# Two attention preparations ahead of the fourth GDN head, and an attend with two score banks, in a two-layer hybrid backbone

## The chip, the cores and the metric

The kernel runs on one core of one Trainium2 chip, as one program. The metric is the time of one execution in microseconds on the device; of several executions the median is taken. A core has five engines that each run their own instructions in order: TensorE (PE, and PEld for its weight loads), VectorE (DVE), ScalarE (ACT), GpSimd (POOL) and SyncE (SP), which here issues the DMAs. They wait for each other through semaphores.

## The reference

Two layers of a diffusion backbone on 1024 latent tokens and 256 context tokens of width 1024. Each layer normalises and modulates its input, mixes the tokens in three parallel groups of heads from one input projection into one output projection, and ends with an MLP of width 4096. The mixer, cut to what matters:

```python
pl = split_cols(h_lat @ w_in, IN_SIZES)        # and pc, of the context
# 4 GDN heads: chunked delta rule, forward and backward
sol = lax.linalg.triangular_solve(amat, rhs, lower=True, unit_diagonal=True)
...
S, o = lax.scan(step, s0, (u, w, attn, qg, kg, glast))
# RG-LRU, width 256, forward and backward: h = a*h + u along the tokens
a = jnp.exp(log_a);  u = jnp.sqrt(-jnp.expm1(2.0 * log_a)) * (i * xc)
# 4 attention heads with latent keys and values; context queries read context keys only
s = jnp.einsum('bqhd,bkhd->bhqk', q, k).astype(jnp.float32) * ((MLA_NOPE + MLA_ROPE) ** -0.5)
p = jax.nn.softmax(s, axis=-1)
y_lat = jnp.concatenate([gdn_out(...), rl * gelu(...), a_l], axis=-1) @ w_out
```

Context outputs of the mixer are computed in layer 0 only.

## The kernel before

All matrices lie with features on the partitions and tokens along the free axis. The tokens stand in three blocks: two of 512 latent tokens (0 and 1) and one of 256 context tokens ("c"). Most float32 products are made of three passes on a high and a low part (tiles "wh" and "wl").

`mixer` writes one layer's work in this order. After the projections for each group (`tiles(h)`: the keys, queries, values and gate of GDN head h), `head(h)` runs GDN head h; heads 0 to 2 are written among the projections. Then come `head(3)`, `mla_open` (the loads of what the attention shares), `mla_prep` 0, the LRU, `mla_prep` 1, `mla_attend` 0, `mla_prep` 2, `mla_attend` 1, `mla_prep` 3, the loads of the mixer's results, `mla_attend` 2 and 3, and the output projection.

- A **GDN head** has an opening (from L591: keys times keys and keys times queries, decays); `gdn_invert`, which inverts 32 x 32 triangles by 60 small VectorE operations on tiles X and T between two pairs of transposes (L681 to L690) and joins them by small matmuls; `gdn_scan`, a recurrence over ten chunks of 128 tokens in two directions, forward with PSUM bank "a" and backward with bank "b", whose last step is an addition to its output X from bank "c" (L790 is the last matmul); and `gdn_y`, which normalises (L821), and gates and stores the output.
- An **attention preparation** (`mla_prep`) computes head h's keys K, queries Q (with the rotary embedding), the row maxima of the scores (matmul L984, VectorE reduction L985, L987) and values V. Preparations 0 and 1 use banks "st" and "d", 2 and 3 "st" and "b". K and V have two buffers each, taken by h modulo 2.
- An **attend** (`mla_attend`) runs over two latent query blocks with ten key chunks each, and over the context block (two chunks) in layer 0. For each chunk there are three score matmuls (L1014 to L1016), an exponential on ScalarE, and a value matmul into bank "d" (L1029); at the end of a block there is a reciprocal (L1031). A score tile takes one of the two "mm" banks; every third one takes bank "a".
- Each chunk also calls `tick(1)`, which may do one step of work that has been put by: in layer 0 these are adaLN products that are needed behind the mixer (`ada_pe`, L273, in bank "c"), each with a load of 512 KB into the two-buffer tile "wr".
- The **LRU** (`lru`, from L826) has 20 segments of 256 tokens a layer: five token blocks, two halves of the width and two directions. A segment is a chain over ScalarE, VectorE and GpSimd: gate activations, an integer seed for an inverse square root (L862), two Newton steps that alternate between GpSimd and VectorE, and a scan instruction along the tokens (L875 forward, L878 backward) that begins from the last value of the segment before it. Its tiles ("lr", with 14 buffers of tag "L") lie in pool mp.

The order in which each engine gets its instructions isn't the order of the text. A scheduler takes, for each engine, what can go next by priority, and priority follows the order in which the program writes the work; `later()` puts back the counter behind a block, so that what follows the LRU has the same priorities as the LRU itself. So the LRU is mixed with whatever is written behind it. On the chip each engine runs its list in order.

```python
self.flip = (self.flip + 1) % 3
ps = (self.MM() if self.flip else self.PT("a"))[:, :n]
```

Of the kernel before, what the change touches and what calls it, by code (L numbers as in the profile page):

```python
# [43 lines left out]
class Trunk:  # L44
# [954 lines left out]
            self.act(V[:, c0:c0 + w, 0:64], ps[:, :w * 64].rearrange("p (c d) -> p c d", d=64))  # L999
        return K, Q, V  # L1000

    def mla_attend(self, h, kqv, with_ctx, yd):

        nc = self.nc
        K, Q, V = kqv
        sc = 96.0 ** -0.5
        hp = 64 * (h % 2)

        def scores(b, b2, i, p):
            n = BLK[b][1]  # L1010
            k = K[b2][:, :, i * P:(i + 1) * P]
            self.flip = (self.flip + 1) % 3
            ps = (self.MM() if self.flip else self.PT("a"))[:, :n]
            nc.tensor.matmul(ps, k[0:97, 0, :], Q[b][0:97, 0, :], start=True, stop=False)  # L1014
            nc.tensor.matmul(ps, k[0:96, 0, :], Q[b][0:96, 1, :], start=False, stop=False)
            nc.tensor.matmul(ps, k[0:96, 1, :], Q[b][0:96, 0, :], start=False, stop=True)  # L1016
            self.act(p, ps, AF.Exp, scale=sc)
        for b in [0, 1] + (["c"] if with_ctx else []):
            chunks = [(b2, i) for b2 in (BL if b != "c" else ["c"]) for i in range(GRP[b2][1])]
            s, n = BLK[b]  # L1020
            po = self.PT("d")[:, :n]
            for ci, (b2, i) in enumerate(chunks):
                c = GRP[b2][0] + i
                self.tick(1)
                if ci % 2 == 0:
                    pt = self.wp.tile([P, 2, 512], F32, tag=("wl", "wh")[ci // 2 % 2], bufs=2, name=self.nm("Pt"))
                p = pt[:, ci % 2, :n]
                scores(b, b2, i, p)
                nc.tensor.matmul(po, V[:, c, :], p, start=ci == 0, stop=ci == len(chunks) - 1)  # L1029
            rc = self.T()[0:64, :n]  # L1030
            nc.vector.reciprocal(rc, po[64:128, :])  # L1031
            self.tt(rc, po[0:64, :], rc, ALU.mult)
            nc.sync.dma_start(yd[hp:hp + 64, s:s + n], rc)

    def mixer(self, L, hs, obl):

        nc = self.nc
        l, last = L.l, L.l == DEPTH - 1
# [3 lines left out]
        yd = [self.dram(f"y{i}") for i in range(8)]  # L1042
# [36 lines left out]
        def head(h):  # L1079
            with self.actor("g", (gp, 2), ["c"]):  # L1080
                o = self.gdn_head(L, h, *kd[h], last)
                self.gdn_y(o, kd[h][1][1], zd[h], obl, yd[h])
# [23 lines left out]
        self.lw = mp.tile([P, 2, 2, 2, P], F32, name=self.nm("lw"))  # L1106
        nc.sync.dma_start(self.lw, self.I["lru_w"][l])
        mq = self.pool("mq", side)
        head(3)
        self.cur = ("s", (self.tp, 4), ["st", "d"])  # L1110
        self.mla_open(L, pk, mq, not last)
        kqv = [self.mla_prep(L, 0, mq, not last)]
# [2 lines left out]
            self.lru(L, [x for x, _ in xg], [g for _, g in xg], obl, yd[4:6])  # L1115
        self.cur = mine
        kqv.append(self.mla_prep(L, 1, mq, not last))
        self.cur = ("s", (self.tp, 4), ["st", "b"])
        self.mla_attend(0, kqv[0], not last, yd[6])
        kqv.append(self.mla_prep(L, 2, mq, not last))  # L1120
        self.mla_attend(1, kqv[1], not last, yd[6])
        kqv.append(self.mla_prep(L, 3, mq, not last))
# [316 lines left out]
```

## Time and profile before

| | |
|---|---|
| time, median of 3 runs (us) | 3834.12 (3833.47 to 3840.0) |
| profiled execution: time, span (us) | 3833.43, 3831.6 |
| mean granted TensorE clock | 0.958 |
| TensorE, VectorE, ScalarE, GpSimd busy | 91%, 55%, 43%, 34% |
| layer 0: head 3's L681, end of its scan, last attend's last reciprocal (us) | 630.5, 747, 1001 |
| layer 1: the same (us) | 2635.2, 2747, 2977 |

The span is divided by the profile into instructions with a start, a length, the engine, the line of the kernel, the operation, and the tiles (out<-in). A stretch's busy time is the union of an engine's instructions in it. An idle time before an instruction is shown in brackets with what ended it. Names of one letter or two are tiles; "lr" are all tiles of the LRU.

### The profile page before, as it was taken

The numbers are of one execution on the slowest core, as the hardware profiler recorded it, in microseconds if no ns is written. First come the engines' busy times: TensorE is split into PE (matmuls) and PEld (weight loads), VectorE is DVE, ScalarE is ACT, GpSimd is POOL, SyncE is SP. The second block draws the span as 40 slices with busy tenths as digits, with TensorE's granted clock in tenths as the row PEclk, the third lists the DMA queues.
The fourth block names the chain that finished last, engine by engine and source line by source line (L and its number), as shares of the span: only waits on it lengthen the run. The fifth ranks groups of instructions, "written<-read, shape, count | busy, mean of one in ns | idle before, by whom it ended". The sixth has DMA issues, their size and how long they took to land. (4 is left out here: it accounts for less than half of the span.)

```text
span 3831.6 us, 51475 instructions
## 1 busy us (share of the span) xinstructions
PE 3501.0 (91%) x19236; PEld 2746.6 (72%) x19236; DVE 2093.5 (55%) x4351; ACT 1645.2 (43%) x3477; POOL 1310.3 (34%) x919
## 2 busy tenths in 40 slices
PE   5999986898999999999997989897887999999998
PEld 3777774645787888888877777774544778888886
DVE  6666577756365155555256685677766361421224
ACT  3554544545454322122354454554555453222242
POOL 4212212235575211111465322112244674222254
PEclk9999998899999999999998999997998999999999
DMA  5221213151532222222434322212002432311143
GB/s 184 93 92 60 93 60 93 34 161 44 175 105 89 66 83 94 88 94 89 130 107 138 99 81 78 86 65 74 31 27 81 153 105 94 96 47 47 51 139 99
DMA packets 164922, 347.13 MB, mean 91 GB/s; under 512 B 15552, under 2 KB 74304, under 8 KB 164672
## 3 DMA queue, kind: packets, MB, share of 16 engines
q1 hardware_dynamic: 164672, 343.85, 27.7%
q8 instruction: 151, 2.47, 0.3%
q14 instruction: 99, 0.81, 0.1%
HBM read 277.99 MB, written 65.80 MB: 90 GB/s over the span
## 5 line engine op out<-in xcount | busy, mean ns | idle before, releaser
L138 POOL TENSOR_TENSOR wl<-wr,wh 128x1024 fp32r<-128x1024 f32 x280 | 682.4, 2438 | 1630.0 <-ACT wh L135 951.7
L230 PE MATMUL mm<-A,wh 128*128 128x512 f32 (+1 forms) x3008 | 704.3, 377 | 11.8 <-DVE A L138 5.4
L135 ACT ACTIVATE wh<-wr 128x1024 fp32r<-128x1024 f32 x288 | 304.9, 1059 | 855.5 <-PE mm L230 332.5
L230 PEld LDWEIGHTS mm<-A,wh 128*128 128x128 f32 x3008 | 521.6, 193 | 107.2 <-DVE A L138 7.3
L138 DVE TENSOR_TENSOR hid<-T,hid 128x512 fp32r<-128x512 f32 (+1 forms) x160 | 172.4, 1080 | 451.9 <-ACT hid L135 451.9
L230 PE MATMUL mm<-A,wl 128*128 128x512 f32 (+1 forms) x1504 | 353.5, 371 | 1.2 <-DVE wl L138 1.1
L230 PE MATMUL mm<-hid,wh 128*128 128x512 f32 (+1 forms) x1280 | 301.8, 377 | 8.8 <-ACT T L135 6.8
L230 PEld LDWEIGHTS mm<-A,wl 128*128 128x128 f32 x1504 | 259.6, 191 | 48.1 <-DVE wl L138 1.3
L230 PEld LDWEIGHTS mm<-hid,wh 128*128 128x128 f32 x1280 | 227.3, 190 | 56.3 <-ACT T L135 7.3
L138 DVE TENSOR_TENSOR acc<-acc,mm 128x512 f32<-128x512 f32 (+1 forms) x140 | 88.5, 632 | 217.0 <-PE mm L230 216.4
L147 DVE SCALAR_TENSOR_TENSOR T<-raw,sm,T 128x512 f32<-128x512 f32 (+4 forms) x240 | 176.5, 737 | 47.8 <-ACT T L135 24.0
L230 PE MATMUL pd<-A,wh 128*128 128x512 f32 (+1 forms) x704 | 195.1, 406 | 0.0
L230 PE MATMUL plr<-A,wh 128*128 128x512 f32 (+1 forms) x800 | 185.7, 383 | 0.0
L1029 PE MATMUL pd<-Pt,V 128*128 128x512 f32 (+1 forms) x336 | 168.7, 627 | 16.9 <-ACT Pt L135 9.7
L135 ACT ACTIVATE T<-T 128x512 f32<-128x512 f32 (+1 forms) x243 | 141.6, 583 | 92.7 <-DVE T L147 69.8
L138 POOL TENSOR_TENSOR S<-S,T 128x512 f32<-128x512 f32 (+1 forms) x126 | 162.5, 1292 | 38.4 <-ACT T L135 35.3
L230 PE MATMUL mm<-hid,wl 128*128 128x512 f32 (+1 forms) x640 | 167.3, 379 | 8.1 <-DVE wl L138 8.1
L230 PE MATMUL pb<-A,wh 128*128 128x512 f32 (+1 forms) x800 | 173.0, 367 | 1.2 <-ACT wh L135 1.2
L147 DVE SCALAR_TENSOR_TENSOR ada<-wa,sil,ada 128x256 f32<-128x256 f32 x392 | 166.4, 488 | 6.6 <-DMA wa<-in_w_ada_dram 6.6
L230 PEld LDWEIGHTS plr<-A,wh 128*128 128x128 f32 x800 | 143.6, 188 | 31.8 <-issue 0.5
L230 PE MATMUL plr<-hid,wh 128*128 128x512 f32 (+1 forms) x640 | 155.8, 386 | 10.1 <-DVE hid L138 10.0
L147 DVE SCALAR_TENSOR_TENSOR lr<-lr,lr 128x256 f32<-128x256 f32 x218 | 108.3, 507 | 100.1 <-POOL lr L138 83.9
(382 smaller groups left out, 6822.5 us busy)
## 6 DMA issues: line engine op xcount, KB each, us to landing
wr<-in_w_mlp_dram SPq DMA_DIRECT2D x208, 512.0 KB, 3.5
wa<-in_w_ada_dram SPq DMA_DIRECT2D x96, 512.0 KB, 3.7
wr<-in_w_in_dram SPq DMA_DIRECT2D x48, 512.0 KB, 3.6
wr<-in_w_out_dram SPq DMA_DIRECT2D x32, 512.0 KB, 3.7
A<-y SPq DMA_DIRECT2D x32, 256.0 KB, 4.0
xm<-acc SPq DMA_DIRECT2D x32, 256.0 KB, 3.8
x<-xm SPq DMA_DIRECT2D x16, 512.0 KB, 6.4
kT<-k SPq DMA_DIRECT2D x8, 640.0 KB, 4.0
```

The costliest lines, as they stand in the source:

```text
L135: return self.nc.scalar.activation(out, in_, f, **kw)
L138: return (eng or self.nc.vector).tensor_tensor(out, a, b, op=op)
L147: return self.nc.vector.scalar_tensor_tensor(out, a, s, b, op0=op0, op1=op1)
L230: mm = nc.tensor.matmul(ps, w[wi][:, wk, :], a[:, ai, :], start=n == 0, stop=n == last)
L1029: nc.tensor.matmul(po, V[:, c, :], p, start=ci == 0, stop=ci == len(chunks) - 1)
```

## The change

`head(3)` moves from before `mla_open` to behind preparation 1, and attend 0 takes its score tiles from the two "mm" banks only. Head 3's own loads, the LRU, the other preparations and the other attends are written as they were.

```diff
@@ -999,7 +999,8 @@
             self.act(V[:, c0:c0 + w, 0:64], ps[:, :w * 64].rearrange("p (c d) -> p c d", d=64))
         return K, Q, V
 
-    def mla_attend(self, h, kqv, with_ctx, yd):
+    def mla_attend(self, h, kqv, with_ctx, yd, third=1):
 
         nc = self.nc
         K, Q, V = kqv
@@ -1010,7 +1011,7 @@
             n = BLK[b][1]
             k = K[b2][:, :, i * P:(i + 1) * P]
             self.flip = (self.flip + 1) % 3
-            ps = (self.MM() if self.flip else self.PT("a"))[:, :n]
+            ps = (self.PT("a") if third and not self.flip else self.MM())[:, :n]
             nc.tensor.matmul(ps, k[0:97, 0, :], Q[b][0:97, 0, :], start=True, stop=False)
             nc.tensor.matmul(ps, k[0:96, 0, :], Q[b][0:96, 1, :], start=False, stop=False)
             nc.tensor.matmul(ps, k[0:96, 1, :], Q[b][0:96, 0, :], start=False, stop=True)
@@ -1106,7 +1107,6 @@
         self.lw = mp.tile([P, 2, 2, 2, P], F32, name=self.nm("lw"))
         nc.sync.dma_start(self.lw, self.I["lru_w"][l])
         mq = self.pool("mq", side)
-        head(3)
         self.cur = ("s", (self.tp, 4), ["st", "d"])
         self.mla_open(L, pk, mq, not last)
         kqv = [self.mla_prep(L, 0, mq, not last)]
@@ -1115,8 +1115,10 @@
             self.lru(L, [x for x, _ in xg], [g for _, g in xg], obl, yd[4:6])
         self.cur = mine
         kqv.append(self.mla_prep(L, 1, mq, not last))
+        head(3)
         self.cur = ("s", (self.tp, 4), ["st", "b"])
-        self.mla_attend(0, kqv[0], not last, yd[6])
+        self.mla_attend(0, kqv[0], not last, yd[6], 0)
         kqv.append(self.mla_prep(L, 2, mq, not last))
         self.mla_attend(1, kqv[1], not last, yd[6])
         kqv.append(self.mla_prep(L, 3, mq, not last))
```

First place: VectorE, layer 0, at the start of head 3's inversion. Of before (X and T_6163 are the inversion, T_67xx, K and Q belong to preparation 0):

```order
1009 L681 STREAM_TRANSPOSE X_6114<-C_6113 128x1024
1010 L138 TENSOR_TENSOR T_6765<-T_6765,T_6767 32x512
1011 L682 MEMSET X_6114 128x32
1012 L138 TENSOR_TENSOR T_6163<-X_6114 128x30
1013 L138 TENSOR_TENSOR T_6779<-T_6779,raw_6736 32x512
1014 L138 TENSOR_TENSOR X_6114<-X_6114,T_6163 128x30
1015 L138 TENSOR_TENSOR K_6777<-pd_6801,K_6777 64x512
1016 L138 TENSOR_TENSOR T_6163<-X_6114 128x58
1017 L138 TENSOR_TENSOR T_6779<-T_6779,T_6781 32x512
1018 L138 TENSOR_TENSOR X_6114<-X_6114,T_6163 128x29x2
```

Of the changed kernel at the same step of the inversion (X and T_7300; lr and pv are the LRU, here its segments 5 and 6):

```order
1133 L681 STREAM_TRANSPOSE X_7251<-C_7250 128x1024
1134 L875 SCALAR_TENSOR_TENSOR lr_6335<-lr_6334,pv_6289,lr_6328 128x256
1135 L147 SCALAR_TENSOR_TENSOR lr_6370<-lr_6371,lr_6370 128x256
1136 L876 COPY pv_6359<-lr_6335 128x1
1137 L682 MEMSET X_7251 128x32
1138 L138 TENSOR_TENSOR T_7300<-X_7251 128x30
1139 L138 TENSOR_TENSOR X_7251<-X_7251,T_7300 128x30
1140 L138 TENSOR_TENSOR T_7300<-X_7251 128x58
1141 L147 SCALAR_TENSOR_TENSOR lr_6370<-lr_6371,lr_6370 128x256
1142 L138 TENSOR_TENSOR X_7251<-X_7251,T_7300 128x29x2
```

The inversion's first transpose moves from row 1009 to row 1133. Both preparations' maxima and the first five LRU scans now stand ahead of it or directly at it, and LRU segments stand among its small operations, where those of preparation 0 stood.

Second place: VectorE, layer 0, in head 3's scan. Of before (X, with gv and vt, is the head's scan; mx is preparation 1's maxima):

```order
1192 L985 TENSOR_REDUCE mx_7765<-pst_7784 128x1
1193 L147 SCALAR_TENSOR_TENSOR X_997_6406<-pb_6553,gv_632,vt_5984 128x128
1194 L985 TENSOR_REDUCE mx_7765<-pd_7787 128x1
1195 L147 SCALAR_TENSOR_TENSOR X_997_6406<-X_997_6406,gv_633,pa_6546 128x128
1196 L985 TENSOR_REDUCE mx_7765<-pst_7790 128x1
1197 L147 SCALAR_TENSOR_TENSOR X_997_6406<-pa_6567,gv_632,vt_5984 128x128
1198 L147 SCALAR_TENSOR_TENSOR X_997_6406<-X_997_6406,gv_633,pb_6560 128x128
1199 L985 TENSOR_REDUCE mx_7765<-pd_7793 128x1
1200 L985 TENSOR_REDUCE mx_7765<-pst_7796 128x1
```

Of the changed kernel, from the fourteenth LRU scan on:

```order
1294 L878 SCALAR_TENSOR_TENSOR lr_6701<-lr_6700,pv_6647,lr_6694 128x256
1295 L879 COPY pv_6725<-lr_6701 128x1
1296 L147 SCALAR_TENSOR_TENSOR lr_6733<-lr_6740,lr_6733 128x256
1297 L147 SCALAR_TENSOR_TENSOR X_1264_7543<-pb_7578,gv_632,vt_7121 128x128
1298 L147 SCALAR_TENSOR_TENSOR lr_6738<-lr_6738,lr_6741 128x256
1299 L147 SCALAR_TENSOR_TENSOR X_1264_7543<-X_1264_7543,gv_633,pa_7571 128x128
1300 L147 SCALAR_TENSOR_TENSOR lr_6701<-lr_6701,lr_6702 128x256
1301 L862 TENSOR_SCALAR lr_6740<-lr_6739 128x256
1302 L138 TENSOR_TENSOR X_7542<-X_7542,pc_7574 128x128
1303 L147 SCALAR_TENSOR_TENSOR X_1264_7543<-pa_7592,gv_632,vt_7121 128x128
1304 L147 SCALAR_TENSOR_TENSOR X_1264_7543<-X_1264_7543,gv_633,pb_7585 128x128
1305 L147 SCALAR_TENSOR_TENSOR lr_6740<-lr_6741,lr_6740 128x256
```

Where the reductions of preparation 1 stood, LRU segments now stand. The last row of head 3's scan (X with bank "c") is row 1233 before, behind the third LRU scan, and row 1384 of the changed kernel, behind the twentieth. In layer 1 it is row 3319 before, behind the third, and row 3471 now, behind the nineteenth. From L681 to that row there stand 15 LRU scans in layer 0 and 14 in layer 1.

Third place: TensorE, layer 0, in the adaLN steps. Of before, in attend 0 (L1014 to L1016 are scores, L1029 value products):

```order
2834 L1029 MATMUL pd_7982<-Pt_7987,V_6749 128x512 x2
2835 L273 MATMUL pc_7872<-wa_7936,sil 32x512 x2
2836 L1029 MATMUL pd_7982<-Pt_8008,V_6749 128x512
2837 L273 MATMUL pc_7872<-wa_7947,sil 32x512 x2
2838 L1029 MATMUL pd_7982<-Pt_8008,V_6749 128x512
2839 L1015 MATMUL pa_8030<-Q_6831,K_6763 128x512
2840 L1016 MATMUL pa_8030<-Q_6831,K_6763 128x512
2841 L1014 MATMUL mm_8040<-Q_6831,K_6763 128x512
2842 L1015 MATMUL mm_8040<-Q_6831,K_6763 128x512
2843 L1016 MATMUL mm_8040<-Q_6831,K_6763 128x512
2844 L847 MATMUL plr_7209<-lr_7207,lw_5955 128x256
2845 L1029 MATMUL pd_7982<-Pt_8029,V_6749 128x512
```

Of the changed kernel, directly behind head 3 (L1015 to L1017 are its scores of attend 1):

```order
2906 L1016 MATMUL pa_8365<-Q_6955,K_6004 128x512
2907 L1017 MATMUL pa_8365<-Q_6955,K_6004 128x512
2908 L273 MATMUL pc_7872<-wa_7894,sil 32x512 x2
2909 L1015 MATMUL pa_8390<-Q_6968,K_5980 128x512
2910 L1016 MATMUL pa_8390<-Q_6968,K_5980 128x512
2911 L1017 MATMUL pa_8390<-Q_6968,K_5980 128x512
2912 L273 MATMUL pc_7872<-wa_7905,sil 32x512 x2
2913 L273 MATMUL pc_7872<-wa_7915,sil 32x512 x2
2914 L273 MATMUL pc_7872<-wa_7926,sil 32x512 x2
2915 L273 MATMUL pc_7872<-wa_7936,sil 32x512 x2
```

From row 2912 on, 13 steps of L273 stand one behind the other with no scores between them, where before one or two stood between the scores. On SP's queue 22 of the 24 loads "wa" stand behind the store of head 3's output.

## The prediction

> **What bounds the kernel now.** I read the busy shares first, then the table by stretches around head 3 in both layers, then VectorE's timeline at the edges of these stretches, then its groups and its waits for the LRU. In the page, TensorE is the busiest engine:
>
> ```profile
> PE 3501.0 (91%) x19236; PEld 2746.6 (72%) x19236; DVE 2093.5 (55%) x4351; ACT 1645.2 (43%) x3477; POOL 1310.3 (34%) x919
> ```
>
> That is an average. The table by stretches (start and end, length, then PE, PEld, DVE, ACT and POOL busy with counts, TensorE clock, DMA share, GB/s) shows what the part that changes is limited by:
>
> ```profile
> 606.00:747.00 141.00, 101.30 (x776) 71.61 (x774) 115.98 (x268) 70.50 (x183) 44.68 (x49) 0.82 0.15 44
> 630.00:691.00 61.00, 34.46 (x92) 21.12 (x93) 54.99 (x118) 17.40 (x36) 18.03 (x19) 0.64 0.02 7
> 747.00:1001.00 254.00, 229.23 (x793) 124.54 (x793) 160.12 (x288) 138.49 (x311) 108.50 (x139) 0.96 0.34 107
> 2605.00:2747.00 142.00, 104.24 (x763) 72.00 (x762) 114.14 (x272) 68.19 (x179) 35.44 (x37) 0.78 0.17 53
> 2747.00:2977.00 230.00, 190.72 (x601) 110.47 (x599) 142.97 (x253) 130.52 (x290) 108.09 (x139) 0.90 0.18 53
> ```
>
> From 606 to 747 us (layer 0) and from 2605 to 2747 us (layer 1) head 3 runs, with the two preparations beside it: VectorE is 0.82 and 0.80 busy, TensorE less. From there to the end of the last attend TensorE leads, 0.90 and 0.83 busy, and VectorE falls to 0.63. The edges, in VectorE's timeline (start, length, operation):
>
> ```profile
> 630.49 1.91 DVE L681 STREAM_TRANSPOSE X<-C 128x1024 f32<-128x1024 f32 x1 [1.00 <-ACT C L135]
> 746.98 0.29 DVE L138 TENSOR_TENSOR X<-X,pc 128x128 f32<-128x128 f32 x1
> 1000.99 1.76 DVE L1031 RECIPROCAL T<-pd 64x256 f32<-64x256 f32 x1 [1.46 <-PE pd L1029]
> 2635.20 1.93 DVE L681 STREAM_TRANSPOSE X<-C 128x1024 f32<-128x1024 f32 x1 [1.18 <-ACT C L135]
> 2746.66 0.29 DVE L138 TENSOR_TENSOR X<-X,pc 128x128 f32<-128x128 f32 x1 [1.18 <-PE pc L790]
> 2977.25 3.36 DVE L1031 RECIPROCAL T<-pd 64x512 f32<-64x512 f32 x1 [12.26 <-PE pd L1029]
> ```
>
> L681 opens head 3's inversion, the last X<-X,pc ends its scan (with it, bank "a" comes free for the attends), the last reciprocal ends the last attend. So there are three stages: A, to L681; B, inversion and scan; C, from the scan's end to the last attend.
>
> Where the LRU lies matters most. Its own scans, one for each of 20 segments a layer:
>
> ```profile
> 748.15 0.74 DVE L875 TENSOR_TENSOR_SCAN lr<-lr,pv,lr 128x256 f32<-128x256 f32 x1
> 958.48 0.75 DVE L878 TENSOR_TENSOR_SCAN lr<-lr,pv,lr 128x256 f32<-128x256 f32 x1
> 2753.42 0.75 DVE L875 TENSOR_TENSOR_SCAN lr<-lr,pv,lr 128x256 f32<-128x256 f32 x1
> 2944.49 0.75 DVE L878 TENSOR_TENSOR_SCAN lr<-lr,pv,lr 128x256 f32<-128x256 f32 x1
> ```
>
> In both layers the first of each pair is the fourth scan and the second is the twentieth: 16 steps in 210.3 us and in 191.1 us, 13.1 and 11.9 us each, nearly all in stage C, beside TensorE's attends, where VectorE has time left.
>
> **The change, part by part.** The order of the changed program puts head 3's inversion behind both preparations and behind LRU segment 5, and all of segments 6 to 20 before the end of head 3's scan. VectorE runs its rows in order, so the LRU leaves stage C and goes into stages A and B. That is what I price; the moved loads of head 3 keep their place on SP's queue.
>
> Stage A grows. Groups of VectorE from 606 to 747 us (count, busy us, mean ns, idle before):
>
> ```profile
> L138 DVE TENSOR_TENSOR X<-X,T 128x30 f32<-128x30 f32 (+14 forms) x30 | 13.2, 441 | 0.3
> L138 DVE TENSOR_TENSOR T<-X 128x30 f32<-128x30 f32 (+14 forms) x30 | 12.7, 424 | 0.3
> L689 DVE STREAM_TRANSPOSE C<-X 128x1024 f32<-128x1024 f32 x1 | 1.9, 1937 | 0.0
> L147 DVE SCALAR_TENSOR_TENSOR X<-pa,gv,vt 128x128 f32<-128x128 f32 x9 | 3.1, 349 | 0.2
> L147 DVE SCALAR_TENSOR_TENSOR X<-X,gv,pa 128x128 f32<-128x128 f32 x8 | 2.8, 346 | 1.7 <-PE pa L780 1.6
> L138 DVE TENSOR_TENSOR X<-X,pc 128x128 f32<-128x128 f32 x10 | 2.8, 283 | 0.0
> ```
>
> The inversion is 60 operations, 25.9 us, and three transposes of 1.9 us, 5.7 us. The scan is 3.1 and 2.8 us for bank "a", as much for "b", and 2.8: 14.6 us. Together 46 us of the 116 that VectorE works in the stretch; the other 70 are the opening of head 3 and the preparations. Behind these stand segments 4 and 5 and the rest of 3, and the end of preparation 1. A segment is about 3.75 us of VectorE by these rows and the scans above (five stt of 0.51, one of L862 at 0.32, scan 0.75, copy 0.15):
>
> ```profile
> L147 DVE SCALAR_TENSOR_TENSOR lr<-lr,lr 128x256 f32<-128x256 f32 x90 | 44.6, 507 | 45.8 <-POOL lr L138 35.8 <-ACT lr L135 9.6
> L862 DVE TENSOR_SCALAR lr<-lr 128x256 int32<-128x256 int32 x16 | 5.1, 321 | 15.2 <-POOL lr L143 15.2
> ```
>
> That gives 70 + 11 + about 6 for the end of preparation 1 (estimate) = 87 us, at 0.82 busy 106 us: L681 at 712 instead of 630. Layer 1, the same without its context queries, 82 us at 0.80: 2707 instead of 2635. TensorE, 101 us busy in the whole first stretch with inversion and scan, does not lead there.
>
> Stage B is disputed. VectorE's own work in it is 46 us for head 3, with some 3 for copies beside it, and 15 segments at 3.75, 56 us: 105 us. Were that all, the scan would end some 112 us behind L681. But the segments stand one behind the other in VectorE's rows: the scan of one, then the Newton steps of the next, each with a round through GpSimd. The wait rows above say that this is slow: 46 and 15 us of idle time in front of these operations, nearly all for GpSimd. One segment, near 870 us, VectorE and then GpSimd:
>
> ```profile
> 871.93 0.94 DVE L878 TENSOR_TENSOR_SCAN lr<-lr,pv,lr 128x256 f32<-128x256 f32 x1
> 874.64 0.93 DVE L147 SCALAR_TENSOR_TENSOR lr<-lr,lr 128x256 f32<-128x256 f32 x1 [1.47 <-POOL lr L138]
> 877.57 1.60 DVE L147 SCALAR_TENSOR_TENSOR lr<-lr,lr 128x256 f32<-128x256 f32 x3 [1.99 <-POOL lr L138]
> 879.28 0.75 DVE L878 TENSOR_TENSOR_SCAN lr<-lr,pv,lr 128x256 f32<-128x256 f32 x1
> ```
> ```profile
> 871.93 0.85 POOL L143 TENSOR_SCALAR lr<-lr 128x256 f32<-128x256 f32 x1 [1.03 <-ACT lr L135]
> 873.88 2.28 POOL L138 TENSOR_TENSOR lr<-lr,lr 128x256 f32<-128x256 f32 x3
> 876.81 1.41 POOL L138 TENSOR_TENSOR lr<-lr,lr 128x256 f32<-128x256 f32 x2
> ```
>
> From one LRU scan to the next is 7.35 us here, with nothing between but the LRU. The bound from below is thus 7.4 us a segment, that from above the mean of 11.9 to 13.1 us beside the attends. In stage B each segment has 46/15, some 3 us, of head 3's operations between its own; some fall into the waits, some behind them. I take 10 us, nearer to the undisturbed chain. Layer 0: 15 segments, 150 us, end of the scan at 862 (before 747: **+115**). Layer 1: 14 until the scan's end and 3 us, 143 us, at 2850 (before 2747: **+103**). The ends for the range: 112 us (VectorE's work alone) and 179 to 196 us (the upper rate).
>
> Stage C shrinks. What is left in it are three attends, preparations 2 and 3 and, in layer 0, the adaLN work of line 273. The length of an attend with nothing of the LRU beside it is read from its reciprocals:
>
> ```profile
> 966.17 1.76 DVE L1031 RECIPROCAL T<-pd 64x256 f32<-64x256 f32 x1
> ```
>
> From this, the end of attend 2, to the last at 1000.99 is 34.8 us. In layer 1, I take 33 (no context block, and no loads for it). A preparation is some 18 us of TensorE, 16.5 in layer 1 (estimate from the stretch before 747). Line 273 is 24 steps of 1.05 us; in the new order 13 of these stand in a run directly behind the scan, each waiting for 512 KB into two buffers:
>
> ```profile
> wa<-in_w_ada_dram SPq DMA_DIRECT2D x96, 512.0 KB, 3.7
> 783.78 1.05 PE L273 MATMUL pc<-wa,sil 128*32 128x512 f32 x4
> 785.82 1.05 PE L273 MATMUL pc<-wa,sil 128*32 128x512 f32 x4
> ```
>
> Two steps in a row start 2.04 us apart, and a load lands after 3.7 us with a short wait for its buffer, so 2.0 to 2.5 us a step: 13 × 1.45 = 19 us at the upper end. Layer 0: 105 + 36 + 25 + 19 + 8 for head 3's output and the start = 193, before 254: **−61**. Layer 1: 99 + 33 + 16 (head 3's output, and the 12 us wait in the last row above) = 148, before 230: **−82**. Ends: 141 (TensorE's work with line 273 hidden) to 236, and 135 to 170.
>
> The second part, two score banks in attend 0, lets its scores and value products run beside preparation 1 and the inversion, where TensorE has room (34 of 61 us busy, second row of the first table); its 33 to 35 us are what stage C loses by it. The other attends keep three banks. Without this edit attend 0 would wait for head 3's scan. With two banks its scores have less lead over the exponentials; that costs nothing while VectorE sets the end of stage A.
>
> Sum: layer 0 +115 − 61 = +54, layer 1 +103 − 82 = +21, **+75 us** on the profiled execution's 3833.43 us (span 3831.6; 1.8 us lie around it): **3908 us**. The median of the three runs is 3834.12, 0.7 us from it, and within their spread.
>
> One thing could make it worse. In the inversion, VectorE, then GpSimd:
>
> ```profile
> 655.31 0.40 DVE L138 TENSOR_TENSOR T<-X 128x228 f32<-128x228 f32 x1
> 656.08 1.44 DVE L138 TENSOR_TENSOR X<-X,T 128x228 f32<-128x228 f32 x1
> ```
> ```profile
> 656.01 1.26 POOL L138 TENSOR_TENSOR Q<-T,Q 32x512 fp32r<-32x512 f32 x1 [2.84 <-ACT Q L135]
> ```
>
> The step that began 0.07 us behind a GpSimd operation took 1.44 us where its neighbour took 0.40, and ended 0.25 us behind GpSimd's. The Trainium skill, "SBUF — State Buffer", section "Who interferes with whom", says that a VectorE instruction with two inputs in SBUF contends with a GpSimd instruction that reads SBUF; this row agrees with it. By this rule the sum would be the one of the first rival, without it the forecast.
>
> **The rivals.** *Lockstep with GpSimd.* The inversion in stage B lies beside six LRU segments, each with seven or eight GpSimd operations of 0.74 us on average (2.28/3 and 1.41/2 in the rows above), 33 us; if VectorE and GpSimd exclude each other through the inversion, and later beside the scan's stt with SBUF inputs, 13 to 31 us a layer come on top, about 44 in all: 3952 us. For it speaks the row at 656.08; against it, that head 3's operations can fall into the LRU's waits.
>
> *The LRU doesn't pace (faster).* If head 3's operations fall wholly into the waits and the segments overlap, stage B takes VectorE's 112 us: scan end at 824 and 2808 instead of 747 and 2747, with the 61 us that the later L681 brings in. Stage C is then nearer its lower end, 169 and 135. Layer 0 +77 − 85 = −8, layer 1 +61 − 95 = −34: 3791 us. It decides at the period of a segment: it holds where this stays below 7.4 us, and at 7.4 us gains and losses cancel. For it speaks the 7.35 us step; against it, that this step had nothing between, and that the mean was 12 to 13.
>
> *Gains and losses cancel.* The period is 7.4 us, or stage C falls to its lower end with 8.5 us a segment: 3834 us within 8.
>
> **How the numbers follow.** Forecast 0.63, lockstep 0.15, cancel 0.08, faster 0.14. Slower is 0.63 + 0.15 = 0.78. About 0.2%, 7.7 us, is what a measurement of this kernel can tell from no change. The range runs from 3826, the lower edge of no change, to 3985, which takes in the lockstep and half the way to the upper rate of a segment (15 × 12 us and the upper end of stage C would give some 4030); the faster case and that end are left out, under 0.2 together. The likeliest case's own range is 3866 to 3960.
>
> **What would show it.** In the changed kernel's profile: L681 near 712 and, with layer 0's 54 us in front, 2761; the LRU scans 9 to 11 us apart between L681 and the end of head 3's scan, with VectorE's idle time ended by GpSimd; that end near 862 and 2904; behind it TensorE over 0.9 busy save in the run of line 273, where DMA ends the waits, and the last reciprocals near 1055 and 3052. It is wrong if the segments step in under 8 us in stage B, if VectorE is over 0.9 busy there, or if stage C shrinks by over 100 us a layer.

## The result, and the profile after

The changed kernel takes 3925.15 us (median of 4 runs, 3920.19 to 3927.54) against 3835.01 us of the kernel before in the same comparison: a ratio of 1.0231, 95% interval 1.0213 to 1.0249, so 82 to 95 us slower. The profiled execution took 3920.19 us, with a span of 3918.4 us, 86.8 us more than the one before.

The edges of the three stages, in VectorE's timeline of the changed kernel (start, length, operation, idle time before it):

```profile
719.11 1.95 DVE L681 STREAM_TRANSPOSE X<-C 128x1024 f32<-128x1024 f32 x1
871.14 0.29 DVE L138 TENSOR_TENSOR X<-X,pc 128x128 f32<-128x128 f32 x1 [0.30 <-PE pc L790]
1072.86 1.76 DVE L1032 RECIPROCAL T<-pd 64x256 f32<-64x256 f32 x1 [1.46 <-PE pd L1030]
2786.28 1.94 DVE L681 STREAM_TRANSPOSE X<-C 128x1024 f32<-128x1024 f32 x1 [0.86 <-ACT C L135]
2934.62 0.28 DVE L138 TENSOR_TENSOR X<-X,pc 128x128 f32<-128x128 f32 x1
3066.08 3.36 DVE L1032 RECIPROCAL T<-pd 64x512 f32<-64x512 f32 x1 [11.00 <-PE pd L1030]
```

Subtracting the same rows of before gives where the time went. Stage A is given as a shift of L681, stages B and C as their lengths before and after, with the forecast shift or length beside them. Layer 1's stage A is what its L681 moved beyond the 71.9 us that layer 0 had already lost.

| stage | layer 0 | forecast | layer 1 | forecast |
|---|---|---|---|---|
| A, to L681 (us) | +88.6 | +82 | +79.2 | +72 |
| B, to the end of head 3's scan | 116.5 to 152.0, +35.5 | 150 | 111.5 to 148.3, +36.9 | 143 |
| C, to the last reciprocal | 254.0 to 201.7, −52.3 | 193 | 230.6 to 131.5, −99.1 | 148 |
| sum | +71.9 | +54 | +17.0 | +21 |

Over both layers the last reciprocal moves by 88.8 us (3066.08 against 2977.25), 2.0 us more than the spans differ by; the rest of the program took that much less.

The three stages of layer 0 and stage B of layer 1 (without its last 1.6 us) by stretches (start and end, length, PE, PEld, DVE, ACT and POOL busy, TensorE clock, DMA share, GB/s):

```profile
606.00:719.00 113.00, 87.68 (x367) 57.57 (x365) 83.03 (x166) 59.77 (x136) 51.39 (x58) 0.74 0.19 59
719.00:871.00 152.00, 107.03 (x641) 74.58 (x641) 111.35 (x255) 84.90 (x221) 84.86 (x115) 0.80 0.16 49
871.00:1073.00 202.00, 175.22 (x584) 85.90 (x584) 89.14 (x136) 66.89 (x141) 21.38 (x17) 0.88 0.32 100
2786.00:2933.00 147.00, 103.09 (x605) 73.24 (x604) 107.65 (x246) 81.41 (x206) 81.65 (x109) 0.76 0.14 43
```

The first two rows show the trouble: no engine is over 0.78 busy for 265 us. VectorE has 111 us of work in stage B, but takes 152 us for it. GpSimd, 0.56 busy there, has little to do in stage C (21 us, 108.5 before): the LRU has gone from beside the attends to beside head 3. Its fifth and twentieth scans:

```profile
720.99 0.70 DVE L875 TENSOR_TENSOR_SCAN lr<-lr,pv,lr 128x256 f32<-128x256 f32 x1
867.63 0.74 DVE L878 TENSOR_TENSOR_SCAN lr<-lr,pv,lr 128x256 f32<-128x256 f32 x1
```

Fifteen steps in 146.6 us are 9.8 us a segment, where the forecast took 10. In layer 1 the sixth and the nineteenth scan start at 2795.32 and 2927.05 us, 10.1 us a segment. VectorE's groups in stage B (count, busy us, mean ns, idle before and what ended it) name what it waits for:

```profile
L147 DVE SCALAR_TENSOR_TENSOR lr<-lr,lr 128x256 f32<-128x256 f32 x84 | 42.4, 511 | 28.5 <-POOL lr L138 26.7 <-ACT lr L135 1.4
L138 DVE TENSOR_TENSOR T<-X 128x30 f32<-128x30 f32 (+14 forms) x30 | 14.2, 473 | 0.3
L138 DVE TENSOR_TENSOR X<-X,T 128x30 f32<-128x30 f32 (+14 forms) x30 | 13.6, 454 | 0.5
```

Of its 40 us of idle time, 26.7 stand before these operations of the LRU and end with GpSimd's.

### The profile page after: what moved, and what is told of

It reads as the page before. It is cut to its first block, busy times and chain, and to the rows that moved or that the text cites. A ratio compares the mean times of both kernels' runs of the same rounds, so it can differ in the third digit from the quotient of the medians.

```text
span 3918.4 us, 51464 instructions
## 1 busy us (share of the span) xinstructions
PE 3545.7 (90%) x19236; PEld 2774.4 (71%) x19236; DVE 2102.0 (54%) x4351; ACT 1647.0 (42%) x3477; POOL 1316.0 (34%) x919
## 5 line engine op out<-in xcount | busy, mean ns | idle before, releaser
L230 PE MATMUL plr<-hid,wh 128*128 128x512 f32 (+1 forms) x640 | 155.7, 386 | 10.2 <-DVE hid L138 10.0
L138 POOL TENSOR_TENSOR lr<-lr,lr 128x256 f32<-128x256 f32 x178 | 132.0, 750 | 71.8 <-DMA lr<-lh 39.4
```

The lines of the kernel that those rows point to most:

```text
L138: return (eng or self.nc.vector).tensor_tensor(out, a, b, op=op)
L230: mm = nc.tensor.matmul(ps, w[wi][:, wk, :], a[:, ai, :], start=n == 0, stop=n == last)
```

## The experiments

**The two parts apart.** First the score banks alone, with head 3 at its old place:

```diff
-        self.mla_attend(0, kqv[0], not last, yd[6])
+        self.mla_attend(0, kqv[0], not last, yd[6], 0)
```

> Only the second part of the change: head 3 stays where it was, attend 0 takes two score banks. Theory (head 3's place is what costs): no change, 3834 within 8 us. Rival (two banks cost attend 0 its lead over the exponentials): up to the 91 us that the changed kernel lost, at least 20 us slower. A gain would say that the third bank made attend 0 wait for head 3's scan and that this wait cost time; at most the time from the first scores to the scan's end that TensorE could use, some 10 us a layer.

Measured: 3836.47 us, ratio 1.0002 (0.9992 to 1.0011). The banks alone show neither a cost nor a gain.

Then the move alone, where attend 0 keeps bank "a" for every third score:

```diff
-        self.mla_attend(0, kqv[0], not last, yd[6], 0)
+        self.mla_attend(0, kqv[0], not last, yd[6])
```

> Only the first part of the change: head 3 behind preparation 1, attend 0 with the third bank as before. Theory: bank a then holds attend 0 back until head 3's scan ends, so that its 33 to 35 us a layer go from beside the inversion to behind the scan; against the changed kernel (3925) +50 to +70 us, less some 10 us a layer for reciprocals that no longer lie ahead of the scan: 3960 to 3990. Rival (the two banks are of no account, or cost time): 3925 or below.

Measured: 3956.71 us, ratio 1.0316 (1.0301 to 1.0331), 32 us above the changed kernel. Its stages B and C, layer 0 and then layer 1:

```profile
716.00:854.00 138.00, 72.61 (x539) 56.67 (x539) 97.17 (x237) 71.21 (x192) 74.93 (x102) 0.67 0.16 48
854.00:1071.00 217.00, 199.73 (x700) 105.52 (x701) 103.05 (x151) 82.69 (x173) 28.29 (x27) 0.95 0.32 97
2795.00:2926.00 131.00, 64.40 (x507) 50.55 (x506) 92.76 (x226) 66.90 (x174) 69.44 (x96) 0.65 0.13 39
2926.00:3102.00 176.00, 158.08 (x524) 91.95 (x525) 90.20 (x131) 77.22 (x154) 28.86 (x29) 0.92 0.14 41
```

Attend 0 goes behind the scan: in layer 1 stage C is 44 us longer, in layer 0 only 14 us. Stage B is 13 and 17 us shorter, but its segments are no faster. The sixth and the nineteenth scan of layer 0:

```profile
719.11 0.75 DVE L875 TENSOR_TENSOR_SCAN lr<-lr,pv,lr 128x256 f32<-128x256 f32 x1
852.58 0.74 DVE L878 TENSOR_TENSOR_SCAN lr<-lr,pv,lr 128x256 f32<-128x256 f32 x1
```

That is 10.3 us a segment, and 10.2 in layer 1, against 9.8 and 10.1 in the changed kernel. Stage B is shorter because fewer scans lie in it, 14 and 13 instead of 16 and 14. Layer 0 gains nothing from the two banks: its last reciprocal starts at 1070.78 us here and at 1072.86 in the changed kernel. One reason shows in TensorE's adaLN steps in layer 0's stage C (count, busy us, mean ns, idle time before and what ended it), first here, then in the changed kernel:

```profile
L273 PE MATMUL pc<-wa,sil 128*32 128x512 f32 x96 | 26.3, 605 | 0.6 <-DMA wa<-in_w_ada_dram 0.6
L273 PE MATMUL pc<-wa,sil 128*32 128x512 f32 x96 | 35.8, 812 | 15.3 <-DMA wa<-in_w_ada_dram 14.6 <-DVE ada L138 0.7
```

With attend 0 behind the scan these steps stand among its scores and hardly wait; with attend 0 ahead of it they stand in a run and wait for their loads. In layer 1, which has no such steps, the two banks are worth 38 us. The result lies just below the range expected.

**Is the LRU's chain what holds head 3?** The two Newton steps, an exchange between GpSimd and VectorE, are left out in both kernels; the LRU's output is then a rough one.

```diff
-            for c in (3.0, 11.978907845725288):
-                self.tt(q, y, y, ALU.mult, gp)
-                self.tt(q, q, wh, ALU.mult, gp)
-                self.stt(y, q, -c, y, ALU.add, ALU.mult)
```

> The changed kernel; every LRU segment leaves out its two Newton steps (four GpSimd and two VectorE operations each), so the LRU's output is only roughly that of the reference. Theory (the segments' chain through GpSimd paces head 3): a segment loses some 4.7 us of chain, 842.0 to 846.7 us in the profile of the changed kernel, so that VectorE's own work, some 95 to 100 us, sets the stretch from L681 to the scan's end instead of 152 and 147 us; all in all 50 to 60 us a layer less, 3805 to 3825. Rival (VectorE's amount of work and the preparations ahead of head 3 are what cost): only 20 us a layer less, the two steps' own VectorE time: 3880 to 3890, stretch at 135.

> The kernel before; every LRU segment leaves out its two Newton steps, as in the other kernel of this pair. Theory: there the segments lie beside the attends, where TensorE is 0.90 and 0.83 busy; 5 to 15 us a layer less, 3805 to 3825, so that the two kernels without these steps lie within 15 us of each other. Rival (head 3's late start costs by itself): 3805 to 3825 as well, but the changed kernel stays 55 us or more above it.

Measured: 3855.39 us (ratio to before 1.0056, 1.0040 to 1.0072) and 3773.69 us (0.9837, 0.9823 to 0.9852): 70 and 61 us less. The stages of the first:

```profile
606.00:722.00 116.00, 91.93 (x373) 59.05 (x373) 83.42 (x168) 66.68 (x152) 40.87 (x42) 0.74 0.20 60
722.00:836.00 114.00, 90.12 (x622) 62.94 (x620) 88.26 (x212) 78.39 (x203) 39.20 (x50) 0.88 0.21 61
836.00:1039.00 203.00, 178.15 (x587) 86.35 (x588) 88.04 (x136) 66.67 (x141) 20.53 (x17) 0.87 0.33 99
```

Stage B falls from 152 to 114 us, 38 us (31 in layer 1), more than the 23 us that VectorE has less to do in it: the amount of its work alone did not hold it. Not all of the 38 us is the shorter chain. Stage A doesn't fall, since the scheduler puts seven LRU scans ahead of L681 instead of four, so 13 scans are left in stage B instead of 16; the period there falls from 9.8 to 8.4 us. Both predictions missed: with the shorter LRU the kernel before gains nearly as much, since its stage C falls as well (254 to 231 and 231 to 196 us). So the LRU's chain costs time in both kernels, and the two still lie 82 us apart, against 90 with the whole chain. The length of the chain accounts for little of the difference between the kernels; that head 3's late start costs by itself, the rival in the second expectation, is nearer to this gap.

**Without the LRU.** Each segment only loads its input and, backward, stores it as the output:

```diff
             nc.sync.dma_start(u, xd[t][:, cs])
-            ps = self.PT("lr").rearrange("p (g n) -> p g n", g=2)
...
+            if d and cs.start >= y0:
+                nc.sync.dma_start(yd[t][:, cs], u)
```

> The changed kernel; the LRU only loads its input and stores it as its output, so that none of its work on the engines is left. Theory (in the changed kernel the preparations and the LRU's segments, at some 10 us each, stand one behind the other ahead of head 3's steps): L681 at 674 as in the kernel with the LRU behind head 3, 45 us earlier than in the changed kernel; from there to the scan's end 95 to 105 us instead of 152 and 147; behind the scan 200 and 133 us as in the changed kernel, since nothing of the LRU lies there. In all 85 to 95 us a layer: 3735 to 3755. Rival (attend 0 beside head 3 makes the inversion and the scan long, by its scores and value products on TensorE): 115 us from L681 to the scan's end, as without the Newton steps: 3765 to 3785.

Measured: 3750.77 us, ratio 0.9775 (0.9752 to 0.9798), 174 us below the changed kernel. Its three stages in layer 0:

```profile
606.00:676.00 70.00, 54.37 (x265) 37.44 (x263) 44.23 (x86) 31.08 (x70) 20.76 (x18) 0.78 0.41 124
676.00:788.00 112.00, 99.02 (x651) 63.71 (x650) 73.85 (x164) 39.05 (x104) 3.95 (x4) 0.85 0.04 11
788.00:991.00 203.00, 176.22 (x586) 86.19 (x587) 88.17 (x135) 66.71 (x141) 20.87 (x16) 0.87 0.33 99
```

L681 at 676 us leaves 45 us of stage A's delay to the two preparations (39 in layer 1); the other 43 us are the LRU's: four to five segments at some 9 to 11 us, not at their 3.75 us of VectorE work. Stage B gives up 40 us in layer 0; in layer 1 it is 105 us and gives up 44. Stage C stays as it was, 203 and 132 us. The total lies in the range expected. Stage B at 112 and 105 us lies above and at the end of its range, and in layer 0 nearer to the rival's 115. TensorE is 99 of 112 us busy there and VectorE 74, so TensorE's work, attend 0's included, is the likelier limit without the LRU; this was not separated.

So the 10 us from one segment to the next in stage B are a pace and not a price. The LRU adds 40 and 44 us to it, some 2.5 and 3.1 us for each of its 16 and 14 scans: most of a segment's time lies beside work that would take 112 and 105 us anyway. In stage A 43 us fall to four to five segments, more than twice their VectorE work.

**The LRU in another place.** It is written behind head 3 instead of ahead of it:

```diff
         kqv = [self.mla_prep(L, 0, mq, not last)]
-        self.cur, mine = self.main, self.cur
-        with self.later():
-            self.lru(L, [x for x, _ in xg], [g for _, g in xg], obl, yd[4:6])
-        self.cur = mine
         kqv.append(self.mla_prep(L, 1, mq, not last))
 
         head(3)
+        self.cur, mine = self.main, self.cur
+        with self.later():
+            self.lru(L, [x for x, _ in xg], [g for _, g in xg], obl, yd[4:6])
+        self.cur = mine
```

> The changed kernel with the LRU written behind head 3 and not ahead of it, so that it lies beside the attends again, as before the change (in the order of VectorE, no scan ahead of L681, eight of twenty ahead of the end of head 3's scan). Theory: L681 comes some 20 us earlier (four to five segments less in the stretch before), the stretch to the scan's end falls to 110 to 120 us, the one behind grows by 10 to 25 us, since the segments lie in it again: in all 35 to 55 us a layer less, 3815 to 3855. Rival (only the later L681 behind two preparations counts): L681 stays at 719 and the sum within 15 us of 3925.

Measured: 3892.41 us, ratio 1.0136 (1.0118 to 1.0154), 33 us less than the changed kernel. Stages B and C in layer 0:

```profile
674.00:809.00 135.00, 111.85 (x691) 73.07 (x689) 100.15 (x230) 69.83 (x180) 43.21 (x59) 0.85 0.09 25
809.00:1036.00 227.00, 184.47 (x630) 96.36 (x630) 135.90 (x239) 108.23 (x242) 89.61 (x110) 0.91 0.37 113
```

The time lies above the range expected (3815 to 3855). L681 comes 45 us earlier, twice what was expected, for the reason just seen. Stage B falls by 17 us only, and stage C grows by 25: eight segments still stand in B, twelve now in C. In layer 1 stage A is 40 us shorter, stage B 25 shorter and stage C 50 longer, 15 us less in all. The eight segments in layer 0's stage B step 18 us apart, so here they don't set its pace; what holds it at 135 us, 22 more than without the LRU, was not separated.

**Shorter waits for the same work.** A scan begins from the last value of the segment before it in its own half of the width and its own direction, so the two halves don't depend on each other. They are written in turn, operation by operation, in both kernels:

```diff
-            for d, t in ((0, 0), (0, 1), (1, 0), (1, 1)):
+            for d in range(2):
                 j = k if d == 0 else k - 5
                 if 0 <= j < 5:
-                    segment(*seq[2 * d + t][j])
+                    g2 = [segment(*seq[2 * d + t][j]) for t in range(2)]
+                    while g2:
+                        g2 = [g for g in g2 if next(g, self) is None]
```

(`segment` has a `yield` between its operations.)

> The changed kernel; the LRU's two halves of the width, which don't depend on each other, are written operation by operation in turn, so that two segments share one chain's waits. The same work, no operation more. Theory (in the inversion and the scan head 3 is held by the segments' waits, and by nothing else that goes away): the stretch from L681 to the scan's end falls from 152 and 147 us to the 114 to 117 us of the kernel without Newton steps or, with VectorE's 15 us more, to 125: 25 to 35 us a layer, 3855 to 3875. Rival (VectorE and GpSimd exclude each other): the same operations lie beside each other, no more than 10 us a layer, 3905 to 3925.

> The kernel before with the LRU's halves in turn, as above. Theory: there the segments' waits hold the stretch behind the scan, which without Newton steps fell by 23 and 35 us; in turn they should give 15 to 30 us a layer, 3775 to 3805, so that the changed kernel stays some 75 us slower with this LRU too, all of it from the later L681. Rival (that stretch is TensorE's, and the LRU beside it costs nothing): within 8 us of 3834.

Measured: 3960.71 us (1.0315, 1.0298 to 1.0333) and 3859.75 us (1.0054, 1.0039 to 1.0069): slower in both, and outside both expectations. VectorE's timeline of the changed kernel with pairs:

```profile
824.77 0.74 DVE L894 TENSOR_TENSOR_SCAN lr<-lr,pv,lr 128x256 f32<-128x256 f32 x1
828.79 0.75 DVE L894 TENSOR_TENSOR_SCAN lr<-lr,pv,lr 128x256 f32<-128x256 f32 x1
844.56 0.81 DVE L894 TENSOR_TENSOR_SCAN lr<-lr,pv,lr 128x256 f32<-128x256 f32 x1
847.67 0.95 DVE L894 TENSOR_TENSOR_SCAN lr<-lr,pv,lr 128x256 f32<-128x256 f32 x1
```

Two segments now end near each other, and then none for 16 us: 20 us from pair to pair, the same 10 us a segment. A pair needs 10 of the 14 "lr" buffers, so the next pair can't begin beside it; that this is the reason was not shown, since there is no room for more buffers. In layer 0 stage B stays at 150 us; most of what the changed kernel loses there lies ahead of L681, which comes 23 us later.

The second attempt takes 1−r out of ScalarE's wait for the Newton steps:

```diff
             self.tt(r, wh, r, ALU.mult, gp)
+            self.tt(u, u, r, ALU.mult, gp)
+            self.act(r, r, AF.Identity, scale=-1.0, bias=one)
...
-            self.tt(u, u, r, ALU.mult, gp)
...
-            self.act(wh, r, AF.Identity, scale=-1.0, bias=one)
...
-            h, a = y, wh
+            h, a = y, r
```

> The kernel before; in each LRU segment u*r and 1-r are taken ahead of the Newton steps, 1-r in place of r and not of the steps' other operand, so that ScalarE need not wait for the steps' end before it goes on to the next segment. The same operations, no one more or less. Theory (the segments are held by the round through ScalarE, GpSimd and VectorE, and hold the stretch behind the scan): a segment of the 13.1 and 11.9 us falls by 1 to 2 us, 10 to 25 us a layer: 3785 to 3820, faster than before. Rival (GpSimd's and VectorE's own order sets the pace): 3835 within 8.

> The changed kernel with the same LRU as in the other kernel of this pair. In the changed kernel ScalarE waits 40 us for GpSimd in the LRU between L681 and the end of head 3's scan. Theory: segments fall from 10 to some 8.5 us in the stretches up to the scan's end, 20 us a layer: 3870 to 3895. Rival: 3925 within 8.

Measured: 3845.52 us (1.0025, 1.0013 to 1.0036) and 3924.96 us (1.0230, 1.0214 to 1.0246). No gain. In the changed kernel the rival holds; the kernel before became some 9 us slower, outside both expectations. ScalarE's waiting for GpSimd in the changed kernel's stage B fell from 40.0 to 29.2 us, its waiting for VectorE in the LRU rose from 2.5 to 8.4. So the 11 us taken from one wait bought nothing; whether the rest of it lies on the chain is not shown.

**The adaLN steps.** Attend 0 calls none:

```diff
-                self.tick(1)
+                if third:
+                    self.tick(1)
```

> The changed kernel; attend 0 calls no adaLN step, so that the 24 steps come from attend 1 on, among its score and value products. Theory (13 steps in a run behind the scan, each waiting for its load, hold TensorE, which is busy 34 of the first 55 us there): 15 to 35 us less in layer 0, nothing in layer 1: 3890 to 3910. Rival (the loads set the pace wherever the steps stand): 3925 within 8.

Measured: 3897.33 us, ratio 1.0150 (1.0134 to 1.0165), 28 us less than the changed kernel. The steps behind the scan in the changed kernel, in TensorE's timeline:

```profile
894.90 1.05 PE L273 MATMUL pc<-wa,sil 128*32 128x512 f32 x4 [1.94 <-DMA wa<-in_w_ada_dram]
897.76 1.92 PE L273 MATMUL pc<-wa,sil 128*32 128x512 f32 x4 [1.81 <-DMA wa<-in_w_ada_dram]
900.21 1.92 PE L273 MATMUL pc<-wa,sil 128*32 128x512 f32 x4 [0.53 <-DMA wa<-in_w_ada_dram]
903.28 1.92 PE L273 MATMUL pc<-wa,sil 128*32 128x512 f32 x4 [1.14 <-DMA wa<-in_w_ada_dram]
```

And stage C of layer 0 without steps in attend 0:

```profile
868.00:1041.00 173.00, 162.89 (x582) 84.17 (x582) 84.96 (x133) 66.50 (x141) 20.59 (x16) 0.98 0.37 116
```

Stage C is 173 us instead of 202. In the run the steps wait for their loads, 2.4 to 3.1 us from one to the next in the rows above, and the matmuls themselves take up to 1.92 us instead of 1.05; the granted clock in stage C is 0.98 without the run and 0.88 with it.

Both edits together, the LRU behind head 3 and no steps in attend 0:

> The changed kernel with the LRU written behind head 3 and with no adaLN steps in attend 0, both of the single edits above together. They act in different stretches, so the sum: 3892 - 28 = 3864 within 10 us, still slower than before, since L681 comes 44 us later by the two preparations alone and the stretch behind the scan pays only part of it back. If instead 3835 or below, the later L681 costs nothing by itself.

Measured: 3883.86 us, ratio 1.0119 (1.0105 to 1.0133). That is 20 us above the sum expected: the edits don't add. The interval overlaps that with the LRU behind head 3 alone, since stage C, 227 us there, falls by 5 us only. What holds it at 222 us, the LRU or the attends, was not separated. No kernel of these with the whole computation beats the one before.

**What stays open.** Of the 90 us between the two kernels the LRU's place is worth 33, the adaLN steps of attend 0 are worth 28, and both together 41. Some 48 us stay with both edits made; L681 then still comes 42 and 41 us a layer later than before, behind the two preparations and no LRU scan. The kernel before was not run without the LRU, so how much the LRU costs there in stage C, and with it how the difference divides between the LRU and head 3's later start, is not settled.

## Why the prediction was right

In the main its mechanism and size held: 3908 us forecast, 3925 measured. The total is closer than its parts. Stages A and B and layer 0's stage C were together 30 us longer than forecast, layer 1's stage C was 16 us shorter, and these errors offset each other in part.

- **Stage A.** Forecast as VectorE's work at the busy share seen before, 712 and, in layer 1, +72 us; measured 719 and +79.2. The total is nearly right, its parts less so: VectorE has 83 us of work there (87 forecast) at a share of 0.73 (0.82 taken). The forecast priced the LRU segments ahead of L681 at 3.75 us each. The runs without the LRU and with the LRU behind head 3 put them at some 9 to 11 us, and the preparations at 45 us (39 in layer 1).
- **Stage B.** 10 us a segment, from the 7.35 us of an undisturbed one and the mean of 12 to 13; measured 9.8 and 10.1 us, and 152.0 and 148.3 us against 150 and 143. The two bounds came from rows; 10 us between them was a choice, and that it came out so exactly is partly luck. Leaving out the LRU takes 40 and 44 us off the stage, leaving out the Newton steps 38 and 31. With the move alone the pace is the same and the stage shorter by the segments that left it. So the segments pace head 3 in the changed kernel; what is not settled is which link of their round through GpSimd and VectorE is decisive, since neither pairing nor ScalarE's earlier release made it shorter.
- **Stage C.** Layer 0 was forecast 9 us too short: the run of adaLN steps was put at 19 us, and the run without it measured 29. Layer 1 was forecast 16 us too long. TensorE is idle for 9 of the 131 us there, nearly all in one wait for ScalarE ahead of head 3's output (L821), where the forecast put 16 us; the other 7 us of these were not lost. TensorE's work is 122 us, where the forecast put 132 for three attends and two preparations.
- **Attend 0.** The forecast let its 33 to 35 us vanish beside stages A and B. The run with the move alone shows 38 us of net gain in layer 1 and none in layer 0, where the run of adaLN steps comes with it. With no steps in attend 0 the last reciprocal of layer 0 starts at 1041.22 us, 30 us ahead of the move alone.
- **Lockstep with GpSimd.** It was priced at 13 to 31 us a layer. In the inversion of layer 0 the two operations went from 424 and 441 ns to 473 and 454 ns, 30 × 62 ns = 1.9 us. The change added little, and the kernel before already had GpSimd beside its inversion, 0.30 busy from 630 to 691 us, against 0.57 from 719 to 780 us now. In the run without the LRU, with GpSimd 0.05 busy from 676 to 737 us, the same 60 operations are 6.7 us shorter than in the changed kernel (the other engines have less to do there too, so that this is GpSimd's doing is argued):

```profile
L138 DVE TENSOR_TENSOR T<-X 128x30 f32<-128x30 f32 (+14 forms) x30 | 10.8, 360 | 0.8
L138 DVE TENSOR_TENSOR X<-X,T 128x30 f32<-128x30 f32 (+14 forms) x30 | 10.3, 344 | 0.8
```

  The larger operations of the preparations in stage A felt more of it, 683 ns before and 1025 ns now, ten of them, 3.4 us:

```profile
L138 DVE TENSOR_TENSOR T<-T,T 32x512 f32<-32x512 f32 x6 | 6.2, 1025 | 0.2
L138 DVE TENSOR_TENSOR T<-T,raw 32x512 f32<-32x512 f32 x4 | 4.1, 1025 | 0.1
```

  Together some 5 us a layer more than before. By the rule of the Trainium skill ("SBUF — State Buffer", "Who interferes with whom") these operations contend with GpSimd's. Both groups agree with it, and the same operations with one input in PSUM (T<-pd,raw) took 692 ns before and now.
- **The faster rival** needed a segment below 7.4 us, and the case that gains and losses cancel 7.4 to 8.5 us; in the changed kernel's stage B it was 9.8 and 10.1 us.

## What to carry to other kernels

An engine works its list in order, so a chain that goes round several engines can set the pace of a list on the critical path that it is mixed into; here a segment of 3.75 us of VectorE work came every 10 us. The pace gives the length of the stage, but not what the chain costs: that is read by leaving it out, and was some 9 to 11 us a segment ahead of L681 and 2.5 to 3.1 us in stage B, where most of its time lay beside other work. Before moving work ahead of a critical chain, read from the new order what comes along with it, and forecast the length by its measured period, not by its busy time. And work that was spread as a filler among matmuls, with its loads, can become a stall of its own when the order lumps it together; here it cost 28 us.

## What the runs showed of the hardware

In these traces TensorE's granted clock follows its occupation, and in the run of adaLN steps this costs time. Layer 0's stage C of the changed kernel, its first 55 us with the run in them and its last 118:

```profile
871.00:926.00 55.00, 33.73 (x91) 7.75 (x90) 8.26 (x22) 9.97 (x33) 0.00 (x0) 0.66 0.49 159
955.00:1073.00 118.00, 114.03 (x412) 69.28 (x411) 67.58 (x86) 52.02 (x100) 18.86 (x15) 0.99 0.19 56
```

At 0.61 busy the clock is 0.66, at 0.97 busy it is 0.99. In the run, where each group waits for a load, four matmuls that take 1.05 us elsewhere take 1.92 us from 897.76 us on. So with waits of 0.5 to 1.8 us come 0.87 us of slower matmuls a step. The Trainium skill, "TensorE: Matmul & The Clock Gate", section "Part 1: The HAM clock gate", says that the clock is gated by how busy the array has lately been; the trace agrees with that here.
